# The start addresses of five weight buffers, modulo 256 bytes, in a one-core diffusion layer

## The chip, the cores and the metric

The kernel runs on one core of a Trainium2 chip. The metric is the device time of one execution in microseconds (us). Before the change the median of three runs is 1443.2 us (1441.6 to 1444.19). The core has a matrix engine (TensorE, PE in the profile; its loads of the stationary operand are listed apart as PEld), VectorE (DVE), ScalarE (ACT), GpSimd (POOL) and SyncE (SP), which issues the DMAs. Data that the engines work on lies in SBUF, 128 partitions wide; a tile's address here is its byte offset within a partition. Matmul results go to PSUM.

## The reference

One layer works on 256 latent tokens and 256 context tokens of width 2048, everything in float32:

```
mod = silu(c) @ w_mod + b_mod          # and the same for the context: shifts, scales, gates
h   = modulate(rms_norm(x),   sh1, sc1);  hc = modulate(rms_norm(ctx), ...)
q, ff, fb, v, g, a, b = split(h @ w_in)   # seven projections of 1024 columns; ctx too
o   = forward + backward gated recurrence per head (8 heads, key and value width 128)
y   = concat(rms_norm(o) * silu(g), silu(layer_norm(conv31(a * sigmoid(b))))) @ w_out
x   = x + g1 * rms_norm(y)
h2  = modulate(rms_norm(x), sh2, sc2)
gate, val = split(h2 @ ffn_up)            # 5632 columns each
x   = x + g2 * rms_norm((gelu(conv3x3(gate)) * val) @ ffn_down)
```

The output is x of the latent tokens.

## The kernel before

A weight of 2048 values per partition (1 MB) comes from HBM into a buffer called raw. The matrix engine computes in a rounded format (fp32r), so each weight is split in two: ScalarE casts raw to the high part whi (line 132), VectorE subtracts and leaves the rest in wlo (line 135). The activations are split in the same way and kept: hT in the heads, y_hi and y_lo for the output projection, h2 for the up projection, hid_hi and hid_lo for the down projection. A product is then three matmuls (high by high, high by low, low by high), or in the up projection two: one of 512 columns that takes both parts of h2 against whi, and one of 256 columns against wlo.

Which operand is stationary and which streams differs by stage:

| stage | lines | stationary | streamed | columns |
|---|---|---|---|---|
| phase 0: adaLN sums, h, the values v | 208 to 210 (v) | hT | vw | 512 |
| heads: ff, fb | 191 to 193 | whi, wlo | hT | 512 |
| heads: q, a, b, g | 191 to 193 | whi, wlo | hT | 256 |
| phase 2: output projection (wo) | 208 to 210 | y_hi, y_lo | whi, wlo; h2 and wroom for some of the last | 512 |
| phase 3: up projection (gate, val) | 199, 200 | whi, wlo | h2 | 512 and 256 |
| phase 4: down projection (dn) | 208 to 210 | hid_hi, hid_lo | whi, wlo | 512 |

In the last quarter of phase 2 weights are also split into room that is free then: into h2, not yet written, and into wroom.

The names h and x in the profile are shorter forms of h2 (and of x0, x1). 88 weights pass through the buffers in the up projection, 44 in the down projection, 48 in the heads, 16 in phase 2.

The buffers lie in a pool that is opened right behind the pool of constants: raw three times, whi three times, wlo twice, taken in turn. In phase 0 the same eight buffers also hold weights of the first adaLN products, unsplit (mraw, line 471). All have 8192 bytes per partition and follow each other, so all eight start at the same offset modulo 256, and what is laid behind them (the pools of vw, v, x1, of the residual tiles, y and hid) starts there too. hT and h2 lie at the other end of SBUF. Every step from one block of 128 or 512 columns to the next within these tiles is a multiple of 256 bytes, so a tile has one offset modulo 256 for all the matmuls that read it.

A scheduler orders the instructions; TensorE's order is held to the written one, in parts of phases 0 and 2 also that of other engines.

Of the kernel before, what the change touches and what calls it, by code (L numbers as in the profile page):

```python
# [8 lines left out]
F32 = mybir.dt.float32  # L9
F32R = mybir.dt.float32r  # L10
U8 = mybir.dt.uint8
ALU = mybir.AluOpType
AF = mybir.ActivationFunctionType
PSUM = bass.MemoryType.PSUM

P = 128
# [8 lines left out]
KB = D // P  # L25
# [15 lines left out]
H2_J = 2  # L41
P0_ENG = {ET.PE, ET.SP}
Y_DG, Y_CX, Y_O, Y_OT, Y_CT = 22, 6.5, 1.5, 6.5, 6
LEVELS = (1, 2, 4, 8, 16, 32, 64)


# [26 lines left out]
class _H2:  # L73


    def __init__(self, k, wo, x1):
        self.k, self.nc, self.wo, self.x1 = k, k.nc, wo, x1
        self.ps, self.ht = {}, {}
# [32 lines left out]
class _Kernel:  # L111
    def __init__(self, tc, a):
        self.tc = tc
        self.nc = tc.nc
        self.a = a
        self.tasks = {}
        self.due = 0
        self.ms = None


    def raw_tile(self, src, prio=600):
# [2 lines left out]
            self.nc.sync.dma_start(raw, src)  # L124
        return raw

    def wtile(self, src, prio=600, hi=None, lo=None):
        raw = self.raws.pop(0) if self.raws else self.raw_tile(src, prio)
        with self.tc.high_priority(prio):
            if hi is None:  # L130
                hi = self.stg.tile([P, 2048], F32R, tag="whi", name="whi", bufs=3)
            self.nc.scalar.copy(hi, raw)  # L132
            if lo is None:
                lo = self.stg.tile([P, 2048], F32R, tag="wlo", name="wlo", bufs=2)
            self.nc.vector.tensor_sub(lo, raw, hi.bitcast(F32))  # L135
        return hi, lo

# [211 lines left out]
    def consts(self):  # L349
        nc, a, cst = self.nc, self.a, self.cst  # L350
        self.params = cst.tile([P, NPAR], F32, name="params")
        nc.sync.dma_start(self.params, a["params"])
        self.ident = cst.tile([P, P], F32, name="ident")
        self.masks = cst.tile([P, 5, 32], U8, name="masks")
        self.onecol = cst.tile([P, 1], F32, name="onecol")
        nc.gpsimd.memset(self.onecol, 1.0)
        self.mhalf = cst.tile([P, 2], F32, name="mhalf")
        nc.gpsimd.memset(self.mhalf, -0.5)


        n = 2 * HEADS
        lg = [self.par("lb", d * n, n) for d in range(DEPTH)]
        mx = cst.tile([P, n], F32, name="lbmx")
        nc.vector.tensor_copy(mx, lg[0])
        for d in range(1, DEPTH):
            nc.vector.tensor_max(mx, mx, lg[d])
        ex = cst.tile([P, DEPTH, n], F32, name="lbex")
        for d in range(DEPTH):
            nc.vector.tensor_sub(ex[:, d, :], lg[d], mx)
        nc.scalar.activation(ex, ex, AF.Exp)  # L370
        sm = cst.tile([P, n], F32, name="lbsm")
        nc.vector.tensor_copy(sm, ex[:, 0, :])
        for d in range(1, DEPTH):
            nc.vector.tensor_add(sm, sm, ex[:, d, :])
        nc.vector.reciprocal(sm, sm)
        for d in range(DEPTH):
            nc.vector.tensor_mul(ex[:, d, :], ex[:, d, :], sm)
        layer = 0
        cum = cst.tile([P, n], F32, name="lbcum")
        nc.vector.tensor_copy(cum, ex[:, 0, :])  # L380
        for d in range(1, layer + 1):
            nc.vector.tensor_add(cum, cum, ex[:, d, :])
        self.lb = cst.tile([P, n], F32, name="lbv")
        nc.vector.tensor_sub(self.lb, cum, ex[:, 0, :])
        self.oml = cst.tile([P, n], F32, name="oml")
        nc.vector.tensor_scalar(self.oml, self.lb, -1.0, 1.0, op0=ALU.mult, op1=ALU.add)


        o = _POFF["cT"][0]
        cc = self.params[:, o:o + 2 * KB]  # L390
        sg = cst.tile([P, 2 * KB], F32, name="csg")
        nc.scalar.activation(sg, cc, AF.Sigmoid)
        self.cs = cst.tile([P, 2 * KB], F32, name="cs")
        nc.vector.tensor_mul(self.cs, cc, sg)

        self.bsc1 = cst.tile([P, KB], F32, name="bsc1")
        nc.vector.tensor_scalar_add(self.bsc1, self.par("bmod", KB, KB), 1.0)
        self.ab = cst.tile([P, 2, KB, 2], F32, name="ab")
        self.mc = cst.tile([P, 4, KB], F32, name="mc")

    def late_consts(self):
        self.nc.sync.dma_start(self.ident, self.a["ident"])
# [9 lines left out]
    def phase0(self, p0, px, srcs):  # L412
        nc, a = self.nc, self.a
# [48 lines left out]
        def gemv_row(q, t):  # L462

            if t == 0:
                rows[q] = px.tile([P, 512], F32, tag="row", name="row", bufs=P0_ROW)
            tag, n = (("raw", 3), ("whi", 3), ("wlo", 2), ("raw", 3), ("whi", 3), ("wlo", 2), ("raw", 3), ("whi", 3))[self.nt % 8]
            self.nt += 1
            w = self.stg.tile([P, 2048], F32, tag=tag, name="mraw", bufs=n)
            nc.sync.dma_start(w, a["wm1"][q, t])
            for g in range(4):  # L470
                nc.tensor.matmul(rows[q][g * 32:(g + 1) * 32, :], cz[:, t * 4 + g, :], w[:, g * 512:(g + 1) * 512],
                                 start=t == 0, stop=t == 3)
            if t == 3:
                r = p0.tile([P, 512], F32, tag="rows", name="rows")
                with self.tc.high_priority(P0_PRIO):
                    nc.scalar.copy(r, rows[q])
                rows[q] = r
# [37 lines left out]
        def v_raw(n, q):  # L515
            raw = p0.tile([P, 1024], F32, tag="vraw", name="vraw", bufs=2)
            nc.sync.dma_start(raw, a["wv"][n, q // 2][:, (q % 2) * 1024:(q % 2 + 1) * 1024])
            return raw
# [56 lines left out]
        for t in range(4):  # L575
            if t == 3:
                self.late_consts()
            gemv_row(0, t)
        self.start_stream(srcs)
        self.order(P0_ENG | {ET.Activation, ET.DVE})  # L580
        raw = v_raw(1, 0)
# [35 lines left out]
        first_s(2, ht)  # L617
        v0(0, 1)
        gemv_row(1, 0)
        tp = first_x(3)  # L620
        ps = v1(0, 2)
        first_s(3, first_m(3, tp))
        v1_add(0, 2, ps)
        gemv_row(1, 1)
        ps = v1(0, 3)
        v1_add(0, 3, ps)
        gemv_row(1, 2)
        gemv_row(1, 3)
        raw = v_raw(1, 1)
# [150 lines left out]
    def head(self, h, st):  # L780
# [22 lines left out]
        kq = [(ks, qs)]  # L803
        for m in LEVELS:
            nb = SEQ // m
# [435 lines left out]
def _pack(inputs):  # L1241
# [32 lines left out]
        [((i[:, None] % 32 // (2 * m) == i[None, :32] // (2 * m)) & (i[:, None] % 32 // m != i[None, :32] // m))  # L1274
         .astype(np.float32) for m in LEVELS[:5]], axis=1)).reshape(P, -1)
    return a
# [13 lines left out]
```

## Time and profile before

| | |
|---|---|
| median of 3 runs | 1443.2 us (1441.6 to 1444.19) |
| the profiled execution | 1439.13 us, span 1437.3 us, mean granted TensorE clock 0.995 |
| TensorE busy | 1400.2 us (97%), 8880 matmuls |
| VectorE busy | 1097.8 us (76%) |
| ScalarE busy | 740.3 us (52%) |
| DMA | 329.21 MB, mean 229 GB/s |

Busy is the time in which an engine has at least one instruction under way. Matmuls overlap: the next starts while the results of the last still leave the array, so a matmul's own length (some 390 ns for 512 columns) is longer than the distance between two starts. A group's line reads: line, engine, operation, what it writes and reads, shape, count, then busy time and the mean length of one, then the idle time before them and what ended it. The chain of waits follows the execution back from its end: each step names the work that the next one had to wait for.

### The profile page before, as it was taken

Reading aid. Unit: us, or ns where it says so; the run is one execution under the profiler, and the core shown is the slowest. Engines: PE = TensorE matmul, PEld = TensorE weight load, DVE = VectorE, ACT = ScalarE, POOL = GpSimd, SP = SyncE. Lnnn points to the kernel's source line nnn. Section 1 sums busy time; section 2 is a strip of 40 time slices with the busy share of each in tenths; the row PEclk is TensorE's granted clock in tenths of the full one; section 3 lists DMA queues with packets and bytes.
Section 4 is the critical chain, followed back from the end, with each engine's and each line's share of the span. In section 5 each row is a group of like instructions: output and inputs, shape, how many; then the busy total and the mean of one; then the engine's idle time right before and its main releaser. Section 6 shows DMA issues by size and latency. Waiting matters only on the chain.

```text
span 1437.3 us, 22182 instructions
## 1 busy us (share of the span) xinstructions
PE 1400.2 (97%) x8880; PEld 1184.3 (82%) x8880; DVE 1097.8 (76%) x1665; ACT 740.3 (52%) x1218; POOL 31.2 (2%) x57
## 2 busy tenths in 40 slices
PE   4999999999999999999999999999999999999997
PEld 2566788888888898888888888888888888888886
DVE  3444788898999988777788888888888887666544
ACT  4333456666666666537655454554545543433531
POOL 0000001001000010000000000000000000000000
PEclk8999999999999999999999999999999999999999
DMA  9988676446644655787355554545555558878653
GB/s 366 385 322 328 254 264 225 162 175 231 235 179 174 222 224 209 291 305 275 122 197 179 194 187 177 199 181 192 190 178 195 184 193 314 331 276 319 235 186 106
DMA packets 49143, 329.21 MB, mean 229 GB/s; under 512 B 5392, under 2 KB 5648, under 8 KB 10896
## 3 DMA queue, kind: packets, MB, share of 16 engines
q1 hardware_dynamic: 49040, 327.80, 61.4%
q8 instruction: 69, 1.13, 0.3%
q14 instruction: 34, 0.28, 0.1%
HBM read 323.58 MB, written 4.19 MB: 228 GB/s over the span
## 4 chain that ended last, share of the span: by engine, by line
PE 77%; DVE 11%; ACT 4%; DMA 3%; issue 2%; POOL 1%; SPq 0%; DVEq 0%; POOLq 0%; ACTq 0%
PE val L199 11%; PE gate L199 11%; PE val L200 6%; PE gate L200 6%; PE dn L210 5%; PE dn L208 5%; PE dn L209 5%; DVE wlo L135 3%; DVE acc L935 3%; PE v L208 2%; PE wo L209 2%; PE wo L208 2%; PE wo L210 2%; PE v L210 2%; PE v L209 2%
## 5 line engine op out<-in xcount | busy, mean ns | idle before, releaser
L135 DVE TENSOR_TENSOR wlo<-raw,whi 128x2048 fp32r<-128x2048 f32 x193 | 441.8, 2289 | 105.1 <-PE dn L209 59.3
L132 ACT CAST whi<-raw 128x2048 fp32r<-128x2048 f32 x193 | 369.5, 1914 | 293.7 <-PE val L199 94.5
L199 PE MATMUL val<-h,whi 128*128 128x512 f32 x704 | 249.0, 393 | 0.0
L199 PE MATMUL gate<-h,whi 128*128 128x512 f32 x688 | 243.4, 393 | 0.0
L200 PE MATMUL val<-h,wlo 128*128 128x256 f32 x704 | 199.1, 283 | 0.0
L200 PE MATMUL gate<-h,wlo 128*128 128x256 f32 x688 | 194.6, 283 | 0.0
L1150 DVE SCALAR_TENSOR_TENSOR gacc<-gate,params,gacc 128x189 f32<-128x189 f32 (+2 forms) x352 | 151.7, 431 | 37.3 <-ACT gacc L1144 29.6
L199 PEld LDWEIGHTS val<-h,whi 128*128 128x128 f32 x704 | 132.2, 188 | 30.5
L199 PEld LDWEIGHTS gate<-h,whi 128*128 128x128 f32 x688 | 129.2, 188 | 29.9
L208 PE MATMUL dn<-whi,hid_hi 128*128 128x512 f32 x352 | 137.4, 390 | 0.0
L210 PE MATMUL dn<-whi,hid_lo 128*128 128x512 f32 x352 | 137.0, 389 | 0.0
L209 PE MATMUL dn<-wlo,hid_hi 128*128 128x512 f32 x352 | 137.0, 389 | 0.0
L200 PEld LDWEIGHTS val<-h,wlo 128*128 128x128 f32 x704 | 132.4, 188 | 0.0
L200 PEld LDWEIGHTS gate<-h,wlo 128*128 128x128 f32 x688 | 129.3, 188 | 0.0
L714 DVE SCALAR_TENSOR_TENSOR big<-graw,cs,big 128x1024 f32<-128x1024 f32 x90 | 113.4, 1279 | 12.7 <-DMA graw<-in_wm_dram 12.1
L935 DVE SCALAR_TENSOR_TENSOR acc<-u,params,acc 128x242 f32<-128x242 f32 (+14 forms) x240 | 98.8, 473 | 0.0
L210 PEld LDWEIGHTS dn<-whi,hid_lo 128*128 128x128 f32 x352 | 66.1, 188 | 13.8
L209 PEld LDWEIGHTS dn<-wlo,hid_hi 128*128 128x128 f32 x352 | 66.1, 188 | 13.7
L208 PEld LDWEIGHTS dn<-whi,hid_hi 128*128 128x128 f32 x352 | 66.1, 188 | 13.4
L208 PE MATMUL v<-vw,hT 128*128 128x512 f32 x128 | 54.1, 423 | 4.1 <-ACT hT L981 3.7
L1154 ACT ACTIVATE ge<-gacc 128x256 f32<-128x256 f32 x44 | 18.5, 419 | 73.8 <-DVE gacc L1150 73.8
L191 PE MATMUL fb<-hT,whi 128*128 128x512 f32 x128 | 53.4, 417 | 0.0
(269 smaller groups left out, 2552.7 us busy)
## 6 DMA issues: line engine op xcount, KB each, us to landing
raw<-in_wup_dram SPq DMA_DIRECT2D x88, 1024.0 KB, 4.8
graw<-in_wm_dram SPq DMA_DIRECT2D x64, 1024.0 KB, 5.0
raw<-in_win_dram SPq DMA_DIRECT2D x48, 1024.0 KB, 5.0
raw<-in_wdn_dram SPq DMA_DIRECT2D x44, 1024.0 KB, 4.8
mraw<-in_wm_dram SPq DMA_DIRECT2D x32, 1024.0 KB, 10.3
raw<-in_wout_dram SPq DMA_DIRECT2D x16, 1024.0 KB, 5.0
vraw<-in_wv_dram SPq DMA_DIRECT2D x16, 512.0 KB, 6.5
x<-in_x_dram SPq DMA_DIRECT2D x2, 1024.0 KB, 9.3
```

The source lines that it names most:

```text
L132: self.nc.scalar.copy(hi, raw)
L135: self.nc.vector.tensor_sub(lo, raw, hi.bitcast(F32))
L191: nc.tensor.matmul(out, wh, xh, start=start, stop=False)
L199: nc.tensor.matmul(ps, hi[:, kb * P:(kb + 1) * P], x, start=start, stop=False, skip_group_check=True)
L200: nc.tensor.matmul(ps[:, :SEQ], lo[:, kb * P:(kb + 1) * P], x[:, 0], start=False, stop=stop, skip_group_check=True)
L208: nc.tensor.matmul(out, xh, wh, start=start, stop=False)
L209: nc.tensor.matmul(out, xh, wl, start=False, stop=False)
L210: nc.tensor.matmul(out, xl, wh, start=False, stop=stop)
L714: nc.vector.scalar_tensor_tensor(self.gacc[:, sl], w[:, sl], c, self.gacc[:, sl], op0=ALU.mult, op1=ALU.add)
L935: nc.vector.scalar_tensor_tensor(d, u[:, lo + o:hi + o], self.par("cw", j * CONVW + k), d, op0=ALU.mult, op1=ALU.add)
L1150: nc.vector.scalar_tensor_tensor(o, g[:, r0 + dy:r1 + dy, c0 + dx:c1 + dx], self.par("fcw", j * 9 + (dy + 1) * 3 + dx + 1), o, op0=ALU.mul ...
L1154: nc.scalar.activation(ge, acc.rearrange("p r c -> p (r c)"), AF.Gelu)
```

## The change

The five buffers of split weights become named slots of one ring each: whi takes slots 0, 1 and 3, wlo slots 2 and 4. Pads of 0, 8, 16, 8 and 8 float32 per partition lie before the slots. The scratch tile csg (32 float32) is dropped, its sigmoid is written to cs in place, and a tile of 16 float32 (cpad) is added to the constants. The raw buffers keep their place in front. The start offsets modulo 256 bytes, as the two programs lay them out:

| tile | before | after |
|---|---|---|
| raw (3 buffers) | 96 | 32 |
| whi (3 buffers) | 96, 96, 96 | 32, 64, 160 |
| wlo (2 buffers) | 96, 96 | 128, 192 |
| vw, v, x0, x1, big, wroom | 96 | 192 |
| y_hi, y_lo, hid_hi, hid_lo | 96 | 192 |
| hT, h2 | 224 | 224 |
| ident | 0 | 0 |
| att, read by the third product of a head (o) as stationary operand | 224 | 224 |
| dg2 (streamed against x1 in the second transposition) | 96 | 192 |

In the up projection gate always takes wlo at 192 and val wlo at 128; whi goes round its three slots. No instruction is added or taken away, and each engine's order and each wait are what they were.

```diff
+SLOTS = {"whi": (0, 1, 3), "wlo": (2, 4)}
+PADS = (0, 8, 16, 8, 8)
...
+        self.turn = {"whi": 0, "wlo": 0}
+        self.slots = []
...
+    def slot(self, kind, dt, name=None):
+
+        ring = SLOTS[kind]
+        i = ring[self.turn[kind] % len(ring)]
+        self.turn[kind] += 1
+        for n in range(len(self.slots), i + 1):
+            if PADS[n]:
+                self.stg.tile([P, PADS[n]], F32, tag=f"pad{n}", name="pad", bufs=1)
+            self.slots.append(self.stg.tile([P, 2048], F32, tag=f"w{n}", name="wslot", bufs=1))
+        return self.stg.tile([P, 2048], dt, tag=f"w{i}", name=name or kind, bufs=1)
...
             if hi is None:
-                hi = self.stg.tile([P, 2048], F32R, tag="whi", name="whi", bufs=3)
+                hi = self.slot("whi", F32R)
             self.nc.scalar.copy(hi, raw)
             if lo is None:
-                lo = self.stg.tile([P, 2048], F32R, tag="wlo", name="wlo", bufs=2)
+                lo = self.slot("wlo", F32R)
...
-        sg = cst.tile([P, 2 * KB], F32, name="csg")
-        nc.scalar.activation(sg, cc, AF.Sigmoid)
         self.cs = cst.tile([P, 2 * KB], F32, name="cs")
-        nc.vector.tensor_mul(self.cs, cc, sg)
+        nc.scalar.activation(self.cs, cc, AF.Sigmoid)
+        nc.vector.tensor_mul(self.cs, cc, self.cs)
...
+        cst.tile([P, 16], F32, name="cpad")
...
-            tag, n = (("raw", 3), ("whi", 3), ("wlo", 2), ("raw", 3), ("whi", 3), ("wlo", 2), ("raw", 3), ("whi", 3))[self.nt % 8]
+            kind = ("raw", "whi", "wlo")[self.nt % 8 % 3]
             self.nt += 1
-            w = self.stg.tile([P, 2048], F32, tag=tag, name="mraw", bufs=n)
+            if kind == "raw":
+                w = self.stg.tile([P, 2048], F32, tag="raw", name="mraw", bufs=3)
+            else:
+                w = self.slot(kind, F32, "mraw")
```

## The prediction

> **What bounds the kernel now.** I read the stage table first, then the chain of waits, then single matmul starts. The table by stage (columns: stretch, its length, then busy time and count of each engine, granted clock, DMA share, GB/s):
>
> ```profile
> core 0: us, PE busy (x) PEld busy (x) DVE busy (x) ACT busy (x) POOL busy (x), PEclk, DMA share, GB/s
> 0.00:161.40 161.40, 141.22 (x736) 89.05 (x736) 80.25 (x155) 62.79 (x104) 3.76 (x12) 0.97 0.87 336
> 161.40:587.60 426.20, 418.85 (x3728) 374.23 (x3729) 383.53 (x714) 269.71 (x599) 23.75 (x39) 1.00 0.58 215
> 587.60:691.10 103.50, 101.86 (x497) 85.34 (x497) 74.30 (x75) 58.01 (x107) 2.59 (x4) 1.00 0.74 279
> 691.10:1185.90 494.80, 494.80 (x2835) 434.25 (x2834) 407.52 (x617) 256.71 (x314) 0.00 (x0) 1.00 0.51 184
> 1185.90:1429.00 243.10, 243.10 (x1090) 201.45 (x1088) 148.71 (x102) 92.39 (x95) 0.55 (x1) 1.00 0.69 255
> ```
>
> The stages are phase 0, the heads, phase 2, up projection (phase 3) and down projection (phase 4). In the last two TensorE is never idle, at full granted clock. The chain inside 691 to 1190 us agrees: TensorE alone.
>
> ```profile
> by line: PE val L199 32.6%; PE gate L199 31.9%; PE val L200 16.9%; PE gate L200 16.5%; PE gate L761 1.2%; PE dn L208 0.3%; PE dn L209 0.3%; PE dn L210 0.2%; PE x2T L84 0.1%
> 691.47 6.01 PE gate L761 x48
> ```
>
> So the question is how long one matmul holds TensorE: the distance from one start to the next. Busy time doesn't tell it, since matmuls overlap; the timeline does (start, length, operation). Four stretches, first and last row of each:
>
> ```profile
> 600.11 0.39 PE L210 MATMUL wo<-whi,y_lo 128*128 128x512 f32 x1
> ...
> 602.83 0.39 PE L210 MATMUL wo<-whi,y_lo 128*128 128x512 f32 x1
> ...
> 657.93 0.39 PE L209 MATMUL wo<-h,y_hi 128*128 128x512 f32 x1
> ...
> 660.25 0.39 PE L210 MATMUL wo<-h,y_lo 128*128 128x512 f32 x1
> ```
> ```profile
> 1250.00 0.39 PE L208 MATMUL dn<-whi,hid_hi 128*128 128x512 f32 x1
> ...
> 1252.72 0.39 PE L208 MATMUL dn<-whi,hid_hi 128*128 128x512 f32 x1
> ...
> 184.34 0.28 PE L192 MATMUL q<-hT,whi 128*128 128x256 f32 x1
> ...
> 186.48 0.28 PE L192 MATMUL q<-hT,whi 128*128 128x256 f32 x1
> ```
>
> The first stretch holds 12 intervals: 2.72/12 = 226.7 ns for 512 columns. The second, ten: 2.32/10 = 232.0 ns. Both are the same three lines of code in the same phase, same width, same type; only the tile that is streamed differs. By the address table, in the first both operands start at 96 modulo 256; in the second, h2 (224) streams against y (96), 128 apart. Down projection (96 against 96): 2.72/12 = 226.7 again. The 256-wide ones of the heads (224 against 96): 2.14/18 = 118.9. In the up projection (224 against 96), 1392 pairs of one 512- and one 256-wide matmul fill 494.8 − 6.0 us: 351.1 ns a pair, which is 232.0 + 118.9 = 350.9. Every matmul of weights 128 apart runs at the slow pace, every one with equal offsets at the fast one.
>
> Plain f32 matmuls of 128 columns, from the chain in order of time, show other offsets:
>
> ```profile
> 60.50 0.87 PE xT L503 x8
> 676.05 1.78 PE x2T L84 x16
> 226.88 1.80 PE o L891 x16
> ```
>
> xT streams ident (0) against x (96): 0.87/8 = 109 ns. x2T (96 and 96): 111 ns. The third (96 and 224): 112 ns. So a pair neither equal nor 128 apart can be at its fast pace, and "equal is fast" holds for the fp32r matmuls alone. I take from this that the pace hangs on where the two read streams of TensorE start, without knowing the rule.
>
> **The change, part by part.** The order of instructions and their waits is the same, row for row, on all five engines. Only addresses move, so every term is a pace times a count. Counts:
>
> ```profile
> L199 PE MATMUL val<-h,whi 128*128 128x512 f32 x704 | 249.0, 393 | 0.0
> L199 PE MATMUL gate<-h,whi 128*128 128x512 f32 x688 | 243.4, 393 | 0.0
> L208 PE MATMUL dn<-whi,hid_hi 128*128 128x512 f32 x352 | 137.4, 390 | 0.0
> L208 PE MATMUL wo<-whi,y_hi 128*128 128x512 f32 x104 | 40.7, 391 | 0.0
> L191 PE MATMUL ff<-hT,whi 128*128 128x512 f32 x128 | 50.6, 395 | 0.7 <-ACT v L687 0.7
> L191 PE MATMUL q<-hT,whi 128*128 128x256 f32 x128 | 36.8, 287 | 0.0
> L208 PE MATMUL v<-vw,hT 128*128 128x512 f32 x128 | 54.1, 423 | 4.1 <-ACT hT L981 3.7
> ```
>
> *Up projection.* Weights go from 96 to 32, 64 or 160 (whi) and 128 or 192 (wlo) against h2, still 224. The 512-wide one can fall by 232.0 − 226.7 = 5.3 ns. No fast 256-wide one is in the trace; half of 226.7 is 113.3, so an estimate of 118.9 − 113.3 = 5.6. All pairs fast: 1392 × 10.9 ns = 15.2 us less. None: 0.
>
> *Heads.* ff and fb: 2 × 3 × 128 = 768 at 5.3 ns = 4.1 us. q, b, a, g: 4 × 3 × 128 = 1536 at 5.6 = 8.6 us. Together 12.7. Here others stand on the chain:
>
> ```profile
> by line: DVE wlo L135 11.1%; DVE acc L935 9.0%; issue 6.5%; DVE big L714 5.0%; PE ff L193 4.6%; POOL rr L231 4.3%; PE ff L191 4.3%; PE ff L192 4.2%; PE fb L191 4.1%; PE fb L193 3.9%; DMA raw<-in_win_dram 3.9%; PE fb L192 3.9%; ACT whi L132
> ```
>
> VectorE's three, issue, GpSimd and the DMA make 39.8%, so I keep 60% of it: 7.6.
>
> *Phase 0.* v: 3 × 128 = 384, from 128 apart to 32 apart (192 against 224): up to 384 × 5.3 = 2.0 us less.
>
> *Output and down projection.* Equal offsets (96/96) become 32, 64, 160, 128 or 192 against 192; only the second wlo buffer stays equal. 3 × 352 + 3 × 104 = 1368 matmuls can lose what they have: 1368 × 5.3 = 7.3 us more. This is the only term known to stand at its good end today.
>
> For the unknown offsets I take half of each span: of the two relations seen in fp32r one is fast and one slow, and of the three f32 rows one. So −15.2/2 − 7.6/2 − 2.0/2 + 7.3/2 = −7.6 − 3.8 − 1.0 + 3.7 = **−8.7 us**. The bounds: all fast −15.2 − 7.6 − 2.0 = −24.8; all slow, with no pace worse than any mean seen, +7.3.
>
> *VectorE and ScalarE* read and write the same buffers, from 96 everywhere to offsets of their own:
>
> ```profile
> L135 DVE TENSOR_TENSOR wlo<-raw,whi 128x2048 fp32r<-128x2048 f32 x193 | 441.8, 2289 | 105.1 <-PE dn L209 59.3
> L982 DVE TENSOR_TENSOR hid_lo<-hd,hid_hi 128x256 fp32r<-128x256 f32 x44 | 18.7, 426 | 20.4 <-ACT hid_hi L981 20.4
> L132 ACT CAST whi<-raw 128x2048 fp32r<-128x2048 f32 x193 | 369.5, 1914 | 293.7 <-PE val L199 94.5
> ```
>
> From 256 to 2048 elements the subtraction grows by 1863 ns, 1.04 ns an element, so neither length shows a stall that a shift could take away by halves; I cost them at nothing. What hides a loss: in the up projection VectorE has 494.8 − 407.5 = 87 us free over 88 subtractions, 1.0 us each; in the heads the cover is 426.2 − 383.5 = 43 us over 48, 0.9 each. Past that every added us is on the path.
>
> *The scratch tile* csg: the sigmoid writes cs and the product is made in place. Same instructions, 32 columns, once, under the first loads: nothing. The raw buffers move from 96 to 32; only DMA, ScalarE and VectorE touch them after phase 0.
>
> *Against the change* stands a rule. The Trainium skill, "TensorE: Matmul & The Clock Gate", section "Step-by-step: what each phase is for", says that loading the next tile's weights takes no read bandwidth from the running matmul; and "SBUF — State Buffer", section "Who interferes with whom", says that "PE and ACT never wait on anyone". By them offsets change nothing and the sum is 0. The rows at 600 and 657 us disagree: 226.7 against 232.0 ns for one piece of code.
>
> **Time.** The profiled execution took 1439.13 us, 1.83 us around its span of 1437.3; 1439.1 − 8.7 = 1430.4. The three runs have a median 4.1 us above it, so on their scale 1443.2 − 8.7 = **1434.5**. Less than 0.2% (2.9 us) is no change that can be measured here.
>
> **Rivals.**
> 1. *All pairs reach the fast pace.* −24.8 us, 1418.4. For it: where offsets are neither equal nor 128 apart the trace has one row (xT), and it is fast. Against: five buffers meet three partners; that all combinations are good is much to ask.
> 2. *Equal is the special case.* Only equal starts give 226.7, any other offset gives 232.0: the output and down projection lose 7.3 us, stages 0, 1 and 3 gain nothing: 1450.5. It decides from the point where fewer than about three in ten of the pairs of the other stages are fast (7.3 lost against 0.3 × 24.8 = 7.4 gained). For it: of the fp32r rows only 96/96 is fast, and that pace is not taken up at once:
>
> ```profile
> 661.61 0.39 PE L208 MATMUL wo<-whi,y_hi 128*128 128x512 f32 x1
> ...
> 662.30 0.40 PE L208 MATMUL wo<-whi,y_hi 128*128 128x512 f32 x1
> ```
>
> These are 96/96 too, straight behind h2's: 0.69/3 = 230 ns. It needs several alike, and with the change whi and wlo, which alternate, no longer start alike. Against: xT. A harder form, with some pairs worse than any mean seen, would also end here: 10 ns more on a third of the 1392 pairs is another 4.6 us, 1455.
> 3. *The tile, not its address, sets the pace.* Streaming h instead of whi differs in more than the start: h2 is one tile written long before, whi three buffers rewritten in turn. Then nothing moves: 1443.2. The page's rule above ends here too. For it: every address pair in the trace goes with one kind of tile. Against: the slow and fast rows of 600 and 657 us share y, PSUM and code. Gain and loss that cancel also end here.
>
> **How the numbers follow.** Forecast (half of each span) 0.54, its own range 1426 to 1441; rival 1 0.15; rival 2 0.17, 0.05 of it the harder form; rival 3 with cancelling 0.14. Faster: 0.51 of the forecast, 0.15, and 0.02 of rival 3: 0.68. Same: 0.03 + 0.10: 0.13. Slower: 0.17 + 0.02: 0.19. The range runs from 1416, under rival 1, to 1449, short of rival 2's price; about 0.07 is left below and 0.12 above.
>
> **What would show it.** In the new profile the up projection's stretch should fall from 494.8 towards 487 us, and pairs should have different lengths by whi buffer, repeating every three tiles, and by gate (wlo at 192) against val (wlo at 128). The down projection's stretch should grow from 243.1 to about 246, with tiles of unequal length where today all are equal. Means of the subtraction and the cast should stay within 10 ns of 2289 and 1914. The forecast is wrong if the down projection gets shorter, if pairs stay at 351 ns in all six combinations, or if the heads gain nothing while pairs there are faster.

## The result: 0.26% slower, and the profile after

The changed kernel takes 1444.64 us (median of 20 runs, 1442.7 to 1446.81), the kernel before 1440.37 us in 20 runs beside it (1438.55 to 1444.19). The ratio is 1.0026 with the interval 1.0019 to 1.0033, 3.7 us slower (the medians differ by 4.3), where 8.7 us faster was forecast. The two profiled spans differ by 6.0 us (1443.3 against 1437.3); stage lengths below are parts of the spans.

The stage table of the changed kernel, in the same five stages and columns as the one before (its stage limits are its own):

```profile
core 0: us, PE busy (x) PEld busy (x) DVE busy (x) ACT busy (x) POOL busy (x), PEclk, DMA share, GB/s
0.00:161.90 161.90, 141.12 (x736) 89.50 (x736) 80.39 (x155) 62.75 (x104) 3.75 (x12) 0.97 0.86 335
161.90:588.70 426.80, 419.04 (x3727) 373.89 (x3728) 383.62 (x714) 268.96 (x598) 23.74 (x39) 1.00 0.57 214
588.70:693.90 105.20, 103.57 (x500) 85.53 (x498) 74.53 (x75) 57.96 (x107) 2.59 (x4) 1.00 0.72 274
693.90:1187.20 493.30, 493.30 (x2835) 432.09 (x2835) 407.19 (x617) 255.83 (x314) 0.00 (x0) 1.00 0.51 185
1187.20:1434.90 247.70, 247.70 (x1090) 201.23 (x1088) 148.46 (x102) 92.03 (x95) 0.55 (x1) 1.00 0.66 251
```

The lengths before, cut by the same first and last matmuls, are 161.5, 426.1, 103.7, 494.8 and 242.9 us. So phase 0 gained nothing (+0.4), the heads gained nothing (+0.7), phase 2 lost 1.5, the up projection gained 1.5 and the down projection lost 4.8. TensorE still has no idle time in the last two stages and the same clock, so this is pace, not waiting.

The groups that carry it (busy, then the mean length of one; the lines are numbered 15 higher than before):

```profile
L150 DVE TENSOR_TENSOR wlo<-raw,whi 128x2048 fp32r<-128x2048 f32 x193 | 441.8, 2289 | 113.9 <-PE dn L224 66.0
L147 ACT CAST whi<-raw 128x2048 fp32r<-128x2048 f32 x193 | 368.6, 1910 | 293.4 <-PE val L214 93.4
L214 PE MATMUL val<-h,whi 128*128 128x512 f32 x704 | 248.3, 395 | 0.0
L223 PE MATMUL dn<-whi,hid_hi 128*128 128x512 f32 x352 | 139.0, 395 | 0.0
```

The subtraction (2289 ns, before 2289) and the cast (1910, before 1914) show no effect of where their buffers start. The matmuls of the down projection went from 390 to 395 ns. What counts there is the distance of their starts; first and last row of a stretch of the changed kernel's timeline:

```profile
1249.69 0.39 PE L223 MATMUL dn<-whi,hid_hi 128*128 128x512 f32 x1
...
1252.47 0.39 PE L223 MATMUL dn<-whi,hid_hi 128*128 128x512 f32 x1
```

Twelve intervals take 2.78 us: 231.7 ns, where the prediction read 226.7 at 1250 us before. Over the whole stage the mean of 1055 intervals is 231.9 ns, before 227.3: 4.6 ns × 1055 = 4.9 us, the whole loss of the stage. In the output projection it is 232.9 against 229.1 over 384: 1.5 us, the loss of phase 2.

In the up projection a pair of one 512- and one 256-wide matmul now has a length for each of the six combinations of buffers. Two tiles of val, on two whi slots, each from its first pair to its last:

```profile
845.53 0.40 PE L214 MATMUL val<-h,whi 128*128 128x512 f32 x1
...
850.83 0.40 PE L214 MATMUL val<-h,whi 128*128 128x512 f32 x1
...
856.76 0.40 PE L214 MATMUL val<-h,whi 128*128 128x512 f32 x1
...
861.97 0.39 PE L214 MATMUL val<-h,whi 128*128 128x512 f32 x1
```

5.30/15 = 353.3 ns and 5.21/15 = 347.3 ns a pair. The six means, each over 210 or 225 intervals within the tiles, are 349.1, 353.3 and 347.1 for val, 351.1, 348.4 and 350.2 for gate; over all 1392 pairs 350.0, before 351.1, where all six were 351.1. 1.1 × 1392 = 1.5 us, the gain of the stage. Address does set the pace, but the mean over six combinations lies close to where it was.

### The profile page after: what moved, and what is told of

The parts are those of the page before. It is cut to its first block, busy times and chain, and to the rows that moved or that the text cites. A ratio compares the mean times of both kernels' runs of the same rounds, so it can differ in the third digit from the quotient of the medians.

```text
span 1443.3 us, 22182 instructions
## 1 busy us (share of the span) xinstructions
PE 1405.1 (97%) x8880; PEld 1182.2 (82%) x8880; DVE 1097.7 (76%) x1665; ACT 738.2 (51%) x1218; POOL 31.2 (2%) x57
## 4 chain that ended last, share of the span: by engine, by line
PE 77%; DVE 11%; ACT 4%; DMA 3%; issue 2%; POOL 1%; SPq 0%; DVEq 0%; POOLq 0%; ACTq 0%
PE val L214 11%; PE gate L214 11%; PE val L215 6%; PE gate L215 6%; PE dn L225 6%; PE dn L223 6%; PE dn L224 5%; DVE wlo L150 4%; DVE acc L953 2%; PE v L223 2%; PE wo L225 2%; PE wo L223 2%; PE wo L224 2%; PE v L225 2%; PE v L224 2%
## 5 line engine op out<-in xcount | busy, mean ns | idle before, releaser
L150 DVE TENSOR_TENSOR wlo<-raw,whi 128x2048 fp32r<-128x2048 f32 x193 | 441.8, 2289 | 113.9 <-PE dn L224 66.0
L147 ACT CAST whi<-raw 128x2048 fp32r<-128x2048 f32 x193 | 368.6, 1910 | 293.4 <-PE val L214 93.4
L732 DVE SCALAR_TENSOR_TENSOR big<-graw,cs,big 128x1024 f32<-128x1024 f32 x90 | 113.3, 1277 | 9.5 <-DMA graw<-in_wm_dram 9.4
```

Source lines behind the costliest of these rows:

```text
L732: nc.vector.scalar_tensor_tensor(self.gacc[:, sl], w[:, sl], c, self.gacc[:, sl], op0=ALU.mult, op1=ALU.add)
```

## The experiments

Two theories stood against each other. *Distance*: the pace follows from where the stationary operand starts against the streamed one, modulo 256, and equal starts are one case among others (my forecast). *Equal is special* (rival 2): equal starts are fast, all others slow. A third, *the tile and not its address* (rival 3), says that moving a tile changes nothing.

Below, d is the start of the stationary operand less that of the streamed one, modulo 256 bytes. Each kernel's d, by the offsets of its tiles:

| kernel | up projection | output and down projection | heads |
|---|---|---|---|
| before | 128 | 0 | 128 |
| after | whi 64, 96, 192; wlo 160, 224 | whi 160, 128, 32; wlo 64, 0 | whi 64, 96, 192; wlo 160, 224 |
| equal | 0 | 0 | 0 |
| uneq | 128 | 96 | 128 |
| all192 | 224 | 0 | 224 |
| ht0 | 224 | 0 | 192 |
| h2only | 224 | 0 | 128 |
| pads0 | 64 | 0 | 64 |

**The pace by offset, alone: map512 and map256.** These leave the layer out: x is loaded and rounded to fp32r, and then TensorE alone runs, 40 matmuls for each of the 64 pairs of starts on a grid of 32 bytes (m is the streamed start, s the stationary one). map512 has 512 columns, and ten pairs off that grid; map256 has 256 columns, and then alternating 512 and 256, as the up projection does.

```diff
+    for m, s in pairs:
+        for k in range(40):
+            nc.tensor.matmul(acc, st(s, k), mov(m, k, 512), ...)
```

> A kernel of matmuls alone: of the layer it keeps nothing but x as data, and its output is not the layer's. One SBUF tile holds x in fp32r; 40 matmuls of 512 columns each, back to back, for every pair of start offsets modulo 256 bytes in steps of 32 (streamed 0 to 224, stationary 0 to 224), and ten pairs with finer steps. Theory 'equal is special': start to start 226.7 ns on the diagonal (streamed = stationary) and some 232 ns everywhere else. Theory 'many offsets are good': about half of the other pairs settle at 226.7 or below as well. Theory 'the tile, not its address, sets the pace': one pace for all 64 pairs.

> As the map of 512 columns (matmuls alone, the output is not the layer's), with 256 streamed columns for 40 matmuls per pair of offsets, then 20 pairs of a 512- and a 256-wide matmul per pair of offsets, as in the up projection. 'Equal is special': 256 columns about 113 ns on the diagonal and 118.9 elsewhere; 512 + 256 about 340 ns on the diagonal, 351 elsewhere. 'Many offsets are good': about half of the others as on the diagonal. 'The tile': one value for all.

Two rows of map512's timeline; equal operations in one piece are one row, with its start, its length and its count. The first lies in the case (32, 32), the second in streamed 32, stationary 64:

```profile
104.05 6.74 PE L48 MATMUL acc<-S 128*128 128x512 f32 x29
...
113.42 6.70 PE L48 MATMUL acc<-S 128*128 128x512 f32 x28
```

Less the last one's 0.39 us, that is 6.35/28 = 226.8 ns and 6.31/27 = 233.7 ns from start to start. The whole map in ns, the median of the eight cases of each d, each over its last 24 intervals (12 for pairs). In map512 the eight cases of one d agree within 0.2 ns, but for d = 128 (232.1 to 233.3) and the first case of all, which starts with intervals of 427 ns. So on this grid d decides:

```
d                      0     32     64     96    128    160    192    224
512 columns        226.7  233.3  233.3  234.2  232.1  233.3  228.9  233.3
256 columns        120.0  118.3  117.8  117.3  118.6  120.0  117.8  116.7
pair of 512+256    353.3  353.3  353.3  346.7  351.1  350.0  348.9  346.7
```

The 512-wide starts of two pair cases of map256, nine intervals each, the first at d = 96 (streamed 0, stationary 96), the second at d = 0 (32 and 32):

```profile
343.26 0.39 PE L52 MATMUL acc<-S 128*128 128x512 f32 x1
...
346.38 0.39 PE L52 MATMUL acc<-S 128*128 128x512 f32 x1
...
385.87 0.40 PE L52 MATMUL acc<-S 128*128 128x512 f32 x1
...
389.05 0.40 PE L52 MATMUL acc<-S 128*128 128x512 f32 x1
```

3.12/9 = 346.7 ns against 3.18/9 = 353.3. For 512 columns rival 2 is nearly right on this grid: d = 0 is the only fast one, with 192 in between. For pairs it is upside down: d = 0 stands among the worst, and 96 and 224 are best. No distance gives a pair of 340 (226.7 + 113.3): the least is 346.7. The layer's paces stand in the map: 128 has 232.1, 118.6 and 351.1, and before showed 232.0, 118.9 and 351.1.

But d isn't all. Single cases left their row, such as, with 256 columns, 113.3 twice at d = 64 and 120.0 twice at 96, and among the pairs 346.7 once at d = 0 (streamed 0, stationary 0) and 353.3 once at 192. And off the grid equal starts aren't fast: map512's (4, 4), (16, 16) and (48, 48) settled at 239.2, 231.1 and 233.3 ns, while (16, 48) had 226.7.

**Everything equal: equal.** All weights, partners, hT and h2 at 224; a pad of 128 bytes behind the constants of the kernel before.

```diff
+        cst.tile([P, 32], F32, name="cpad")
```

> The kernel before with 128 bytes of padding behind the constants, nothing else: raw, whi, wlo, vw, y, hid all start at 224 modulo 256, as hT and h2 do, so every streamed operand and its stationary one have equal offsets in all stages. 'Equal is special': down projection unchanged (243 us), up projection 1392 x up to 10.9 ns = up to 15 us shorter, heads up to 8, phase 0 up to 2: ratio 0.983 to 0.99. 'The tile': ratio 1.000, up projection 494.8 us as before.

Measured: 1441.99 us against 1440.5, ratio 1.0008 (0.9999 to 1.0018). Its up and down projection:

```profile
693.90:1191.90 498.00, 498.00 (x2835) 432.45 (x2835) 407.78 (x617) 256.29 (x314) 0.00 (x0) 1.00 0.52 183
1191.90:1434.80 242.90, 242.90 (x1089) 201.17 (x1087) 148.44 (x102) 92.29 (x95) 0.55 (x1) 1.00 0.69 255
```

Moving both operands together leaves the down projection at 242.9 us, and equal starts in the up projection make it 3.2 us longer (353.3 ns a pair, as in the map). In total the kernel can't be told from the one before. Equal starts are not good as such.

**Only the down projection made unequal: uneq.** Weights stay at 96, the pools behind them go to 192: d = 96 there, the slowest on the map's grid for 512 columns.

```diff
+    padp, pad = enter(name="pad", bufs=1)
+    pad.tile([P, 24], F32, name="vpad")
...
+    leave(padp)
```

> The kernel before with a pad of 96 bytes behind wlo: the weights all stay at 96, and what lies behind them moves to 192 (vw, v, y, hid). In the output and down projection every weight is now 96 apart from its partner, but all alike, so the relation does not change from matmul to matmul. 'Equal is special': the down projection loses its 226.7 ns pace, 1056 x 5.3 = 5.6 us longer, and 1.7 in phase 2: ratio about 1.004. 'It is the change of relation from whi to wlo that costs': 226.7 ns stays, ratio 1.000.

Measured: 1452.15 us, ratio 1.008 (1.0065 to 1.0095). Its last two stages, and the first and last of 13 matmuls:

```profile
697.00:1191.80 494.80, 494.80 (x2835) 434.20 (x2834) 407.48 (x617) 256.17 (x314) 0.00 (x0) 1.00 0.52 184
1191.80:1442.40 250.60, 250.60 (x1089) 201.98 (x1088) 148.72 (x102) 92.25 (x95) 0.55 (x1) 1.00 0.67 248
```
```profile
1300.08 0.39 PE L208 MATMUL dn<-whi,hid_hi 128*128 128x512 f32 x1
...
1302.89 0.40 PE L208 MATMUL dn<-whi,hid_hi 128*128 128x512 f32 x1
```

2.81/12 = 234.2 ns, as in the map. The up projection, whose d is untouched, keeps its 494.8 to the digit, and the down projection is 7.7 us longer: more than the 5.6 expected, since d = 96 is slower than the 232.0 that the price went by. Phase 2 is 2.3 us longer (106.0 against 103.7). The other 1.7 of the 11.7 us between the medians lie elsewhere; where, no run shows. Rival 3 falls with this: code, tiles and order are those of before and only addresses moved.

**The change without its pads: pads0.** The new kernel with all five slots at one offset again, 32, with its partners at 32 too.

```diff
-PADS = (0, 8, 16, 8, 8)
+PADS = (0, 0, 0, 0, 0)
```

> The change with its five pads set to zero: all weights and what lies behind them at 32, hT and h2 at 224 (distance 64 where weights are stationary, 0 where they stream). 'The distance sets the pace': the down projection is back at 243 us, pairs in the up projection at 353.3 ns, so 498 us; heads little changed: +3 us against the kernel before, ratio 1.002, as slow as the change for another reason. 'Moving the base is harmless and the pads do the harm': ratio 1.000.

Measured: 1443.58 us against 1441.38, ratio 1.0014 (1.0004 to 1.0024). Heads, up and down projection:

```profile
160.40:587.50 427.10, 415.43 (x3727) 368.68 (x3728) 383.50 (x714) 269.21 (x598) 23.74 (x39) 1.00 0.58 214
...
691.20:1189.10 497.90, 497.90 (x2835) 433.03 (x2835) 407.84 (x617) 256.29 (x314) 0.00 (x0) 1.00 0.51 183
1189.10:1432.30 243.20, 243.05 (x1089) 201.25 (x1088) 148.59 (x102) 92.20 (x95) 0.55 (x1) 1.00 0.68 255
```

This splits the change in two. Dropping csg and adding cpad, which moves everything behind by 64 bytes, costs the up projection 3.1 us by itself (d from 128 to 64: 353.3 ns a pair). The pads then gain 4.6 us there (497.9 to 493.3) and lose 4.5 in the down projection (243.2 to 247.7) and 1.5 in phase 2 (103.7 to 105.2).

**One offset chosen by the map: all192, ht0, h2only.** If d is the cause, d = 224 in the up projection and 0 in the down projection should beat both kernels. all192 moves all weights and partners to 192 (h2 stays at 224); ht0 moves hT to 0 besides; h2only leaves all of before and moves h2 alone, from 224 to 128. The remarks are not in the code.

```diff
+        cst.tile([P, 24], F32, name="cpad")           # all192 and ht0, behind the constants
...
+    self.hTp.tile([P, 56], F32, name="hpad")          # ht0, behind hT
...
+    h2.tile([P, 24], F32, name="hpad")                # h2only, behind h2; nothing else
```

> The kernel before with a pad of 96 bytes behind the constants: raw, whi, wlo, vw, y, hid all at 192, hT and h2 at 224. Equal offsets in the output and down projection (226.7 ns kept), stationary minus streamed = 224 modulo 256 in heads and up projection, where the maps give 346.7 for a pair, 233.3 for 512 and 116.7 for 256 columns. Theory 'a distance sets the pace, as the maps say': up projection 1392 x 4.4 ns = 6.1 us shorter; heads 1536 x 2.0 shorter and 768 x 0.9 longer, 60% of 2.4 = 1.4; phase 0 0.4 longer: about 7 us less, ratio 0.995. Theory 'distinct offsets matter, not the distance': no gain, ratio 1.000 as in the kernel with all offsets equal.

> As the one with all at 192, and hT moved to offset 0 by a pad of 224 bytes, so that the distance in the heads is 192, where the maps give 228.9 for 512 and 117.8 for 256 columns (against 232.4 and 118.7 at 128). Theory 'as the maps say': heads 768 x 3.5 + 1536 x 0.9 = 4.1 us of matmul time shorter, 60% of it 2.4; with the up projection's 6.1 about 8 us less, ratio 0.9945. The heads may give less, since VectorE and DMA stand on the chain there.

> The kernel before with h2 alone moved from 224 to 128 by a pad of 96 bytes (distance 224 in the up projection, all else as before). 'As the maps say': pairs at 346.7 instead of 351.1 ns, the up projection's 494.8 us become 488.7, ratio 0.9958. 'Only a layout with five offsets can avoid collisions': no gain.

Measured against 1439.98 us: all192 1435.49, ratio 0.9967 (0.9955 to 0.9979); ht0 1432.85, ratio 0.995 (0.9937 to 0.9963); h2only 1434.06, ratio 0.9956 (0.9945 to 0.9968). All three beat both kernels, and h2only does it with one pad. h2only's last two stages, and its pairs over 18 intervals:

```profile
692.50:1181.10 488.60, 488.60 (x2835) 433.62 (x2835) 404.05 (x616) 254.81 (x314) 0.00 (x0) 1.00 0.52 187
1181.10:1424.00 242.90, 242.90 (x1089) 201.39 (x1088) 148.80 (x102) 92.20 (x95) 0.55 (x1) 1.00 0.68 256
```
```profile
849.79 0.39 PE L199 MATMUL gate<-h,whi 128*128 128x512 f32 x1
...
856.03 0.39 PE L199 MATMUL val<-h,whi 128*128 128x512 f32 x1
```

6.24/18 = 346.7 ns, the map's least, and 1392 × (351.1 − 346.7) = 6.1 us is the whole of 494.8 − 488.6. all192 and ht0 have the same 488.6 and 242.9.

ht0 also bears on the heads' term. The heads stage of all192, then of ht0, and two of ht0's groups in that stage:

```profile
162.10:591.00 428.90, 419.33 (x3728) 372.58 (x3729) 384.44 (x715) 269.01 (x598) 23.72 (x39) 1.00 0.58 213
...
162.90:590.80 427.90, 418.11 (x3727) 374.08 (x3728) 383.74 (x714) 268.81 (x598) 23.74 (x39) 0.99 0.58 214
```
```profile
L191 PE MATMUL ff<-hT,whi 128*128 128x512 f32 x128 | 50.1, 391 | 0.7 <-ACT v L689 0.7
...
L192 PE MATMUL q<-hT,whi 128*128 128x256 f32 x128 | 35.8, 279 | 0.0
```

Before, these were 395 and 287 ns. The median distance of ff's starts fell from 232 to 229 ns and that of q's from 119 to 118, and the stage is 427.9 us against 426.1. In pads0 q's median is 114 ns (d = 64, where the map had 113.3 twice) and the stage is 427.1. Yet this doesn't show that faster matmuls leave the heads as long as they were: each stage length is of one execution, and ht0's profiled one, 1436.24 us, is the slowest of its six runs. all192 differs from ht0 in the pad behind hT alone and has the same lengths from phase 2 on (103.7, 488.6 and 242.9 us). Five of ht0's six runs are faster than every run of all192, by 2.6 us in the medians, where the 60% rule gave 1.0 (2.4 against 1.4). What the heads keep of faster matmuls stays open.

**Where the dependence comes from: mapld.** This also leaves the layer out, and streams one fixed block: against stationary blocks at eight offsets; at distances longer by 256, 512, 1024 and 4096 bytes; with both operands moved by 16; with a stationary operand that is one element read 128 times; and with one of 32 columns.

```diff
+    for s in range(0, 256, 32):
+        go(S[:, 8192 + s // 4:8192 + s // 4 + 1].to_broadcast([P, 128]), mov(0, 0, 512))
```

> Matmuls alone (the output is not the layer's), 512 columns, 40 per case, streamed operand at 0. Five groups of eight stationary offsets: (1) one fixed block; (2) the offsets 0 and 192 plus 256, 512, 1024 and 4096 bytes; (3) both operands moved by 16 bytes; (4) a stationary operand that is one element read 128 times; (5) one of 32 columns instead of 128. Theory 'the load of the next stationary operand and the stream meet in SBUF': (1) as in the first map (226.7 at distance 0, 228.9 at 192, 232 to 234 else); (2) the same as without the addition; (4) and (5) lose most or all of the dependence, since there is nearly nothing to load, and fall below 226.7. Theory 'it is the stream alone that is slow': (4) and (5) as (1).

A row inside the last of the eight cases with one element, and one inside the second of those with 32 columns (d = 32):

```profile
303.71 8.50 PE L48 MATMUL acc<-S 128*128 128x512 f32 x36
...
322.71 8.55 PE L48 MATMUL acc<-S 128*32 128x512 f32 x35
```

In the first, 8.11/35 = 231.7 ns, and all eight cases have 231.7: with one element in place of a block, the offset no longer matters. With 32 columns it still does: 8.16/34 = 240.0 ns at d = 32, slower than any case of whole blocks, and the eight cases have 231.7, 240.0, 231.7, 230.5, 230.7, 233.5, 231.7 and 233.3. So the first theory is right that the dependence hangs on what is read as the stationary operand, and wrong that less to load is faster: neither group falls below the 226.7 of d = 0, and a quarter of the columns keeps the dependence. The load doesn't simply take time from the stream. What mechanism it is stays open.

With whole blocks the map's row for 512 columns comes back in all eight cases. The distances longer by 256, 512, 1024 and 4096 bytes give 226.7 each for d = 0 and 228.9 for d = 192, as without the addition: for these two the period is 256 bytes. Both operands moved by 16 bytes gives another row (231.1, 226.7, 228.9, 226.7, 233.3, 233.3, 226.7, 232.2), so on a finer grid d isn't all here either.

**The finer grid: map16.** The layer is left out again; steps of 16 bytes, streamed at 0 and at 16, to look for a pair below 346.7.

```diff
-    pairs = [(m, s) for m in range(0, 256, 32) for s in range(0, 256, 32)]
+    pairs = [(m, s) for m in (0, 16) for s in range(0, 256, 16)]
```

> Matmuls alone (the output is not the layer's): 512 columns, 256 columns, and pairs of both, for streamed offsets 0 and 16 and stationary offsets 0 to 240 in steps of 16. Moved both by 16 bytes, three of eight distances settled at 226.7 ns with 512 columns. If a few pairs too find such a state, 512 + 256 comes down to 340 ns (226.7 + 113.3) at some offset; if the pair keeps its own best, 346.7 stays the least value seen.

Measured: no pair below 346.7, which ten of the 32 cases reach. Streamed 0 against stationary 32 gives 346.7 here and had 353.3 in map256; streamed 0 against 16 with 512 columns gives 226.7 here and had 233.3 in map512. Same addresses, same instructions, another pace: the addresses alone don't decide between the settled paces. The programs differ in the matmuls that ran before, and they ran on different chips (map256 and map512 on one, map16 on another); no run separates the two. So the map is no table to look up digits in, though the layer agreed with it in each up and down projection.

## Why the prediction was wrong

**The step that failed** is "For the unknown offsets I take half of each span". It took both paces of a pair to be free to be fast, 226.7 + 113.3 = 340, and half of all pairs to get there: −7.6 us. The map shows what a pair can have: 346.7 to 353.3. Against 351.1 before, all 1392 pairs could gain 6.1 us or lose 3.1, not gain 15.2 or lose nothing. Spread over three whi and two wlo slots, the change drew from the middle: by the map's rows for one width (233.3 + 234.2 + 228.9)/3 + (120.0 + 116.7)/2 = 350.5, and 350.0 was measured. The start of the error is that I read one fast and one slow relation as a coin with two sides, and halved a 512-wide price to get a fast 256-wide one that no row showed. The measured 1444.64 us lies within the 1416 to 1449 that I gave, but by the width of that range and not by its sum, which has the wrong sign.

**Output and down projection**, priced +3.7 (half of +7.3), is the same step from the other side. Here the good end was in use, and the map has no second one as good. By the map whi at 160, 128 and 32 averages 232.9, wlo at 64 and 0 averages 230.0; two parts of the first and one of the second give 231.9, and 231.9 was measured. +4.8 and +1.5 us are 6.3 of the 7.3. "Equal is the special case" was right for this term, its sign and nearly its size, and wrong for the up projection, where equal is among the slowest.

**Heads**, priced −3.8: the same step again. The medians of after's starts hardly moved (ff and fb 232 to 233, the 256-wide ones 119 to 118), as the map has it: over the five buffers' d its rows average 232.5 and 117.9, against 232.1 and 118.6 at 128. So there was next to nothing for the second factor, 60%, to be taken of, and the change doesn't test it. That TensorE has some 60% of the chain doesn't show that 60% of a saving passes through; all192 and ht0 leave it open. The heads' lengths over the eight layer kernels run from 426.1 to 429.5 us in one execution each, with no order by matmul pace; whether +0.7 is the change or the execution stays open too.

**Phase 0**, priced −1.0: +0.4 in one execution each. v's median start distance is 234 ns, before 233; d = 32 is slow in the map (233.3) as 128 is (232.1).

**VectorE, ScalarE, the scratch tile**: right, nothing. 2289 and 1910 ns, and VectorE's busy time in the up projection is 407.2 us as against 407.5.

**The marks** I had named: unequal pairs by whi slot and by gate against val, held; unequal tiles in the down projection, held (settled tiles of 230.0 to 232.6 ns, before 226.7 in nearly all); the up projection at 487 us, missed (493.3); the down projection at 246, exceeded (247.7). "The heads gain nothing while pairs there are faster" wasn't put to the test, as the matmuls there got hardly faster.

**The rule against the change**, from the Trainium skill, "TensorE: Matmul & The Clock Gate", section "Step-by-step: what each phase is for", was that a load of the next weights takes no read bandwidth from the running matmul. By it offsets of the stationary operand would change nothing. The same code ran at 226.7 ns in the down projection of before and at 234.2 in uneq's, and in mapld the difference went away with a stationary operand of one element, though not with one of 32 columns. The measurement decides against the rule's consequence for these fp32r matmuls; how the two reads meet, no run here shows.

**Settled by runs**: that addresses alone make the difference (uneq, pads0, h2only), that the down projection lost what equal starts gave, and that the up projection could have gained 6.2 us and got 1.5. **Open**: the mechanism behind d, what else than d chooses the pace off the grid and in the single cases, and the heads.

## What to carry to other kernels

Where TensorE never waits, measure the distance between matmul starts, and treat the start address of each operand modulo 256 as a parameter for each shape of the inner loop: here equal starts were best for runs of 512 columns and near the worst for 512 and 256 in turn. Search it with a small kernel of the same loop, move one tile to the best offset, confirm it in the kernel itself (one pair of addresses had 346.7 ns in one program and 353.3 in another), and leave what already runs at the best pace alone; a spread of offsets buys the mean, and here the best single move (one pad behind h2) gave 0.44%. In a stage where others take turns with the engine, its share of the chain is no measured rate at which savings pass through, and stage lengths from one execution each can't give that rate when the effect is a few us: compare the medians of several runs of kernels that differ there alone.

## What the runs showed of the hardware that I had not expected

- The pace of an fp32r matmul of 512 columns goes from 226.7 to 234.2 ns with nothing but d on a grid of 32 bytes, and for d = 0 and 192 it stays the same when the distance grows by 256 to 4096 bytes. Off the grid equal starts are not fast (239.2 ns at 4 and 4).
- The order of the distances is another one for each shape: d = 0 is the best for 512 columns (226.7), among the worst for 256 (120.0) and for pairs (353.3 against a least of 346.7).
- The pace settles in states: 226.7, 233.3, 346.7, 353.3, 113.3 and 120.0 ns come back again and again. As means they are whole multiples of 6.67 ns (34, 35, 52, 53, 17 and 18 times), and others lie at simple fractions between two of them (228.9 a third of the way, 350.0 half). One pair of addresses settled at 346.7 in one program and 353.3 in another.
- A stationary operand of one repeated element makes the pace the same at eight offsets (231.7 ns), but not the fastest; one of 32 columns keeps the dependence (230.5 to 240.0 ns).
